# Forgetting attention: the decay bias of a whole PSUM bank by one 512-column product, and the gates' running sums in float32r parts

## The chip, the cores and the metric

The kernel runs on one core of a Trainium2 chip. The metric is the device time of one execution in microseconds (us), taken over three runs. Beside them one execution was recorded by the hardware profiler; all durations below come from it.

## The reference

The program is a decoder trunk of two layers on one sequence of 256 positions and 1024 channels, in float32. Each layer is a first SwiGLU step, a mixer and a second SwiGLU step. The mixer projects the normed input once and runs three branches on the result: sparse attention (A), forgetting attention (B) and a gated delta rule (C). Each branch is projected, weighted by its gate, and the sum is projected back.

```
def forgetting_attention(q, k, v, log_f):            # 8 heads of 64
    c = transpose(cumsum(log_f, axis=1), (0, 2, 1))
    def block(args):                                 # 2 blocks of 128 queries
        qb, cb, pb = args
        logits = (einsum('bqhd,bshd->bhqs', qb, k) * d ** -0.5
                  + (cb[..., :, None] - c[..., None, :]))
        causal = pos[None, :] <= pb[:, None]
        p = softmax(where(causal, logits, -inf), axis=-1)
        return einsum('bhqs,bshd->bqhd', p, v)
```

The forget gates `log_f` (8 per position) are summed along the sequence, and the difference of the sums is added to the logits. The term of the query is the same for a whole row of the softmax and drops out of it; so the kernel adds only the key's term, −c[s].

## The kernel before, in words

**Matrix products.** The large products (`pw`, `po` of the SwiGLU steps; `pt`, the mixer's input projection; `pbr`, the branch projections; `pmo`, the output projection) take float32 weights that stream from HBM as `raw` tiles. ACT rounds each to float32r (`hi`) and DVE makes the rest (`lo`); TensorE multiplies hi·hi, lo·hi and hi·lo. These splits are issued at high priority.

**Branches.** `branch_a`, `branch_b` and `branch_c` are Python generators; the products of the projection are emitted one by one, and between them the generators are advanced a step at a time by a running estimate of time (`PACE`, `CP`, the `cost` of each product). The order in which each engine finally takes its instructions is set by a scheduler that simulates the engines. It cannot be read from the text alone: an instruction that was emitted a little later, or estimated a little longer, may end up far from where it was. The gate products (`pt`, six pieces of a 512-column projection) and the branch projections come in the order `SEQ`: gates 0 and 1, branch 0, gates 2, branch 1, branch 2.

**Branch B.** `branch_b` (line 945) first sums the gates: `lf` holds them on positions, and two float32 products with a triangle of ones, `tri1`, put the running sums of all 256 positions into the bank `cc`. DVE rounds them to `cq`, and makes `cr`, in which rows 0 to 7 hold the rounded sums of the 8 heads and rows 8 to 15 the rest, with a second copy at rows 64 to 79. Then `softmax_pv` (line 790) runs three jobs: the first block of queries with all four pairs of heads (128 keys), and the second block with pairs 0 and 1, and with pairs 2 and 3 (256 keys). A job has two banks of logits, `lg`: heads of even number in one, of odd number in the other, 512 columns each. `score` adds one head: a float32 product of q and k on 64 of the 128 rows (`lg<-bqk`; even heads use rows 0 to 63 and odd heads rows 64 to 127), then a float32r product on the same 64 rows that adds −c (`lg<-cr,ohr`), where `ohr` has −1 in the rows of the head. After that come the mask (DVE), the maximum, exp, sum and scaling (`L`, DVE and ACT), in the next steps the transposes of the probabilities (`pT`, copied to `PT` by ACT) and the value products (`pv`, 64-column stationary), and the parts `yh` (ACT) and `yl` (DVE) that the branch projection takes. The pool `pa` has two banks; `cc`, `lg`, `pT` and `pv` share them.

**Branch C.** The delta rule goes through four chunks; its last products are `wv`, added to `X` on DVE. Then ACT squares and sums `X` by head (`junk`, `so`), POOL raises the sum to −1/2, DVE scales `X` eight times, TensorE transposes it (`yc`), and ACT and DVE make its parts `ych` and `ycl`.

In the profile nearly every operation of ACT, DVE and POOL has line 85, every product line 147 and every transpose line 151, since helpers issue them; tiles tell them apart.

Of the kernel before, what the change touches and what calls it, by code (L numbers as in the profile page):

```python
# [9 lines left out]
F32 = mybir.dt.float32  # L10
F32R = mybir.dt.float32r
AF = mybir.ActivationFunctionType
OP = mybir.AluOpType
AX = mybir.AxisListType

P = 128
D = 1024
T = 256
# [15 lines left out]
C_ID, C_TRI, C_MASK, C_MASKT, C_LVL = 0, 128, 384, 640, 768  # L34
C_ROPE = C_LVL + 128 * len(LEVELS)
C_SEL = C_ROPE + 32
C_D16 = C_SEL + 10
C_O16 = C_D16 + 128
C_E16 = C_O16 + 128
N_CONST = C_E16 + 16  # L40
# [153 lines left out]
def trunk_kernel(ctx: ExitStack, tc: tile.TileContext, x, consts, par, rows, bgate, fnorm,  # L194
# [4 lines left out]
    cp = ctx.enter_context(tc.tile_pool(name="cp", bufs=1))  # L199
    rawp = ctx.enter_context(tc.tile_pool(name="rawp", bufs=NR))  # L200
    hlp = ctx.enter_context(tc.tile_pool(name="hlp", bufs=NH))
    wk = ctx.enter_context(tc.tile_pool(name="wk", bufs=2))
# [22 lines left out]
    E = Emit(tc, rawp, hlp, units, NR, NH)  # L225
    V, S, G = E.V, E.S, E.G
# [12 lines left out]
    cst = cp.tile([P, N_CONST], F32, name="cst")  # L239
# [4 lines left out]
    tri1 = cst[:, C_TRI:C_TRI + 2 * P]  # L244
    ones = cst[:, C_TRI + P:C_TRI + 2 * P]
    mask = cst[:, C_MASK:C_MASK + 2 * P]
# [2 lines left out]
    V.memset(mhalf, -0.5)  # L249
    phalf = cp.tile([P, 8], F32, name="phalf")  # L250
    V.memset(phalf, 0.5)
    ohr = cp.tile([P, 8], F32R, name="ohr")
    V.tensor_copy(ohr, cst[:, C_SEL + 2:C_SEL + 10])

    def k4(name, dt=F32):
        return wk.tile([P, 1024], dt, name=name, tag="k4", bufs=K4)
# [16 lines left out]
    def v3(t, a):  # L273
        return t.rearrange("p (a b) -> p a b", a=a)
# [197 lines left out]
    def k2(name):  # L472
        return wk.tile([P, 512], F32, name=name, tag="k2", bufs=K2)

    def tiny(name, n, bufs=2):
        return wk.tile([P, n], F32, name=name, tag="t_" + name, bufs=bufs)

    def rows_bc(r, name):

# [77 lines left out]
    def branch_c(l, qkv, gd, hh, hl, need):  # L557
# [101 lines left out]
        for t in range(2):  # L659
            V.tensor_tensor(half(Z, t).rearrange("p (q k r) -> p q k r", q=4, k=8),  # L660
                            zv[:, 4 * t:4 * t + 4, None, :].to_broadcast([P, 4, 8, 16]),
                            cst[:, None, C_D16:C_D16 + P].rearrange("p o (k r) -> p o k r", k=8).to_broadcast([P, 4, 8, 16]),
                            op=OP.mult)
# [122 lines left out]
            G.tensor_tensor(out=x1, in0=r[0], in1=r[1], op=OP.subtract)  # L786
            G.tensor_tensor(out=x2, in0=r[2], in1=r[3], op=OP.add)

    def softmax_pv(br, bias, score, pv, hh, hl):

        jobs = ((0, 0, 4), (1, 0, 2), (1, 2, 2))
        rows = (slice(0, 64), slice(64, 128))
        pr, ptt = {}, {}

        def logits(j):
            b, p0, npair = jobs[j]
            n = P * (b + 1)
            L = k4("L")  # L800
            lv = L.rearrange("p (h s) -> p h s", s=n)
            nh = 2 * npair
            mx, rs = tiny("mx", 8, 3), tiny("rsum", 8, 3)
            pts = [pa.tile([P, npair, n], F32, name="lg", tag="s") for _ in range(2)]
            for i in range(npair):
                for g in range(2):
                    score(pts[g][:, i, :], rows[g], p0 + i, g, b, i == 0)
            for g in range(2):
                V.tensor_tensor(lv[:, g * npair:(g + 1) * npair, :], pts[g],
                                bias(b)[:, None, :].to_broadcast([P, npair, n]), op=OP.add)  # L810
            V.tensor_reduce(mx[:, :nh], lv, axis=AX.X, op=OP.max, negate=True)
            for h in range(nh):
                S.activation(lv[:, h, :], lv[:, h, :], AF.Exp, bias=mx[:, h:h + 1],
                             accum_out=rs[:, h:h + 1])
            V.reciprocal(rs[:, :nh], rs[:, :nh])
            for h in range(nh):
                S.activation(lv[:, h, :], lv[:, h, :], AF.Copy, scale=rs[:, h:h + 1])
            pr[j] = lv

        def transposes(j):  # L820
            b, p0, npair = jobs[j]
            lv = pr.pop(j)
            ptt[j] = []
            for kb in range(b + 1):
                for h0 in range(0, 2 * npair, 4):
                    pt = pa.tile([P, 512], F32, name="pT", tag="s")
                    for h in range(4):
                        E.tr(pt[:, h * P:(h + 1) * P], lv[:, h0 + h, kb * P:(kb + 1) * P], ident)
                    o = k2("PT")
                    S.activation(o, pt, AF.Copy)  # L830
                    ptt[j].append(o)

        def values(j):
            b, p0, npair = jobs[j]
            pts = ptt.pop(j)
            pt = pa.tile([P, npair, P], F32, name="pv", tag="s")
            for kb in range(b + 1):
                if b == 0:
                    pe, po = pts
                else:  # L840
                    pe, po = pts[kb][:, :2 * P], pts[kb][:, 2 * P:]
                pv(pt, rows, pe, po, p0, npair, kb, kb == 0, kb == b)
            if j == 0:
                hh[br], hl[br] = ktiles("yh", 1)[0], ktiles("yl", 1)[0]
            d = (slice(None), slice(p0, p0 + npair), slice(b * P, (b + 1) * P))
            S.activation(hh[br][d], pt, AF.Copy)
            V.tensor_tensor(hl[br][d], pt, hh[br].bitcast(F32)[d], op=OP.subtract)

        n = len(jobs)
        for i in range(n + 2):  # L850
            if i < n:
                logits(i)
                yield
            if 0 <= i - 1 < n:
                transposes(i - 1)
                yield
            if 0 <= i - 2 < n:
                values(i - 2)
                yield
# [85 lines left out]
    def branch_b(gd, bq, bk, bv, hh, hl, after):  # L945
        E.finish(after)
        pt = pa.tile([P, 512], F32, name="cc", tag="s")
        lf = v3(gd["lf"], 2)
        E.mm(pt[:, 0:T], lf[:, 0, :], tri1, True, False, cost=0.434)
        E.mm(pt[:, P:T], lf[:, 1, :], tri1[:, :P], False, True)  # L950
        cr = wk.tile([P, T], F32R, name="cr", tag="cr", bufs=1)
        cq = wk.tile([P, T], F32R, name="cq", tag="cq", bufs=1)
        ct = wk.tile([P, T], F32, name="ct", tag="ct", bufs=1)
        V.tensor_copy(cq, pt[:, 0:T])
        V.tensor_scalar(ct, cq.bitcast(F32), cst[:, C_SEL:C_SEL + 1], None, op0=OP.mult)
        V.scalar_tensor_tensor(cr, pt[:, 0:T], cst[:, C_SEL + 1:C_SEL + 2], ct,
                                       op0=OP.mult, op1=OP.subtract)
        yield
        qv, kv, vv = v3(bq, 4), v3(bk, 4), v3(bv, 2)

        def score(o, rr, p, g, b, first):
            n = P * (b + 1)
            h = 2 * p + g
            E.mm(o, qv[rr, p, b * P:(b + 1) * P], kv[rr, p, :n], first, False, cost=0.217 * (b + 1))
            E.mm(o, ohr[rr, h:h + 1].to_broadcast([64, P]), cr[rr, :n], False, True, cost=0.109)

        def pv(pt, rows, pe, po, p0, npair, kb, first, last):
            for i in range(npair):
                for g, m in enumerate((pe, po)):
                    h = 2 * (p0 + i) + g  # L970
                    E.mm(pt[rows[g], i, :], vv[:, kb, 64 * h:64 * h + 64], m[:, i * P:(i + 1) * P],
                         first and i == 0, last, cost=0.135)

        yield from softmax_pv(1, lambda b: mask[:, P * (1 - b):], score, pv, hh, hl)

    def mixer(pi, st):
        xt, ssq, tasks = st
# [134 lines left out]
    first = new_xt()  # L1112
# [21 lines left out]
def shape_consts():  # L1134
    c = np.zeros((P, N_CONST), np.float32)
    i = np.arange(P)
    c[:, C_ID:C_ID + P] = np.eye(P)
    c[:, C_TRI:C_TRI + P] = i[:, None] <= i[None, :]
    c[:, C_TRI + P:C_TRI + 2 * P] = 1.0
    c[:, C_MASK + P:C_MASK + 2 * P] = np.where(i[None, :] <= i[:, None], 0.0, NEG)  # L1140
    c[:, C_MASKT:C_MASKT + P] = np.where(i[None, :] >= i[:, None], 0.0, NEG)
    for n, b in enumerate(LEVELS):
        bj, bi = i[:, None] // b, i[None, :] // b
        m = (bj % 2 == 0) & (bi == bj + 1)
        c[:, C_LVL + n * P:C_LVL + (n + 1) * P] = m.T
    c[:, C_D16:C_D16 + P] = i[:, None] // 16 == i[None, :] // 16
    c[:, C_O16:C_O16 + P] = c[:, C_D16:C_D16 + P] - np.eye(P)
    c[:, C_E16:C_E16 + 16] = i[:, None] % 16 == i[None, :16]
    pos = np.arange(T, dtype=np.float32)
    inv = np.power(np.float32(500000.0), -np.arange(0, 16, 2, dtype=np.float32) / np.float32(16))  # L1150
    ang = (pos[:, None] * inv[None, :]).astype(np.float32)
    for t in range(2):
        c[:, C_ROPE + 8 * t:C_ROPE + 8 * (t + 1)] = np.cos(ang[t * P:(t + 1) * P])
        c[:, C_ROPE + 16 + 8 * t:C_ROPE + 16 + 8 * (t + 1)] = np.sin(ang[t * P:(t + 1) * P])
    for r in (0, 64):
        c[r:r + 8, C_SEL] = -1.0
        c[r + 8:r + 16, C_SEL:C_SEL + 2] = 1.0
        for h in range(8):
            c[r + h, C_SEL + 2 + h] = -1.0
            c[r + 8 + h, C_SEL + 2 + h] = -1.0  # L1160
    return c


# [38 lines left out]
```

## Time and profile before

| | |
|---|---|
| three runs | 1135.08, 1137.55, 1138.8 us (median 1137.55) |
| profiled execution | 1136.66 us, span 1134.8 us |
| TensorE (PE) | 1110.2 us busy, 98% |
| VectorE (DVE) | 814.0 us, 72% |
| ScalarE (ACT) | 659.0 us, 58% |
| GpSimd (POOL) | 94.4 us, 8% |
| mean granted TensorE clock | 0.995 |
| HBM | 170 GB/s over the span |

A share of busy time is a mean over stages with different limits. Rows of a timeline give start, length, engine, line, operation, output and inputs, shape; in square brackets stands the idle time of the engine just before, with what ended it. A float32 product appears as two records; ends of products are modelled and overlap, so the pace is read from one start to the next. Layer 0's branch B lies at about 330 to 385 us of the span, layer 1's some 560 us later.

### The profile page before, as it was taken

The numbers are of one execution on the slowest core, as the hardware profiler recorded it, in microseconds if no ns is written. First come the engines' busy times: TensorE is split into PE (matmuls) and PEld (weight loads), VectorE is DVE, ScalarE is ACT, GpSimd is POOL, SyncE is SP. The second block draws the span as 40 slices with busy tenths as digits, with TensorE's granted clock in tenths as the row PEclk, the third lists the DMA queues.
The fourth block names the chain that finished last, engine by engine and source line by source line (L and its number), as shares of the span: only waits on it lengthen the run. The fifth ranks groups of instructions, "written<-read, shape, count | busy, mean of one in ns | idle before, by whom it ended". The sixth has DMA issues, their size and how long they took to land. (4 is left out here: it accounts for less than half of the span.)

```text
span 1134.8 us, 17281 instructions
## 1 busy us (share of the span) xinstructions
PE 1110.2 (98%) x6540; PEld 947.5 (83%) x6540; DVE 814.0 (72%) x1328; ACT 659.0 (58%) x1164; POOL 94.4 (8%) x116
## 2 busy tenths in 40 slices
PE   7999999998999999999999999999999999999997
PEld 6888898897778788888888888989878778788885
DVE  5777579889746676776567766888896557677764
ACT  6665456644758646655456645565647685465643
POOL 0010002100000100100010100030000002010100
PEclk9999999999999999999999999999999999999999
DMA  7666656555434355666656666564554334556662
GB/s 280 192 187 187 188 174 190 166 160 167 151 111 148 119 182 154 202 188 189 188 180 186 186 193 188 170 186 154 165 170 155 103 111 149 182 162 191 187 208 91
DMA packets 56515, 194.08 MB, mean 171 GB/s; under 512 B 6256, under 2 KB 8816, under 8 KB 56432
## 3 DMA queue, kind: packets, MB, share of 16 engines
q1 hardware_dynamic: 56144, 192.46, 54.9%
q8 instruction: 51, 0.84, 0.3%
q10 hardware_dynamic: 288, 0.52, 0.1%
q14 instruction: 32, 0.26, 0.1%
HBM read 191.78 MB, written 1.18 MB: 170 GB/s over the span
## 5 line engine op out<-in xcount | busy, mean ns | idle before, releaser
L85 DVE TENSOR_TENSOR lo<-raw,hi 128x1024 fp32r<-128x1024 f32 (+2 forms) x353 | 444.6, 1260 | 218.1 <-ACT hi L85 214.5
L85 ACT ACTIVATE hi<-raw 128x1024 fp32r<-128x1024 f32 (+2 forms) x353 | 372.7, 1056 | 322.3 <-PE pt L147 86.5
L147 PE MATMUL pw<-xt,hi 128*128 128x512 f32 x1024 | 352.2, 399 | 4.1 <-ACT hi L85 2.5
L147 PE MATMUL pw<-xt,lo 128*128 128x256 f32 x1024 | 265.0, 281 | 0.0
L147 PEld LDWEIGHTS pw<-xt,hi 128*128 128x128 f32 x1024 | 189.9, 189 | 43.0 <-ACT hi L85 3.2
L147 PE MATMUL pt<-hi,xt 128*128 128x512 f32 (+1 forms) x640 | 207.0, 399 | 4.7 <-DVE gate L85 4.7
L147 PEld LDWEIGHTS pw<-xt,lo 128*128 128x128 f32 x1024 | 193.7, 189 | 8.3
L147 PEld LDWEIGHTS pt<-hi,xt 128*128 128x128 f32 x640 | 120.5, 190 | 29.6 <-issue 6.2
L147 PE MATMUL pt<-lo,xt 128*128 128x512 f32 (+1 forms) x320 | 128.4, 401 | 1.7 <-DVE lo L85 1.7
L147 PE MATMUL pt<-xt,hi 128*128 128x256 f32 x640 | 118.0, 286 | 0.0
L147 PE MATMUL po<-hi,hl 128*128 128x512 f32 x256 | 99.9, 390 | 0.0
L147 PE MATMUL po<-lo,hh 128*128 128x512 f32 x256 | 99.7, 389 | 0.0
L147 PEld LDWEIGHTS pt<-xt,hi 128*128 128x128 f32 x640 | 99.1, 191 | 0.4
L147 PE MATMUL po<-hi,hh 128*128 128x512 f32 x256 | 91.1, 390 | 0.0
L147 PE MATMUL pt<-xt,lo 128*128 128x256 f32 x320 | 88.9, 284 | 0.0
L147 PEld LDWEIGHTS pt<-lo,xt 128*128 128x128 f32 x320 | 61.1, 191 | 14.8 <-DVE lo L85 2.6
L85 POOL TENSOR_TENSOR hr<-hg,rbc 128x512 f32<-128x512 f32 x32 | 43.2, 1349 | 313.5 <-DVE hg L85 293.9
L147 PEld LDWEIGHTS pt<-xt,lo 128*128 128x128 f32 x320 | 60.5, 191 | 0.0
L147 PEld LDWEIGHTS po<-hi,hl 128*128 128x128 f32 x256 | 48.1, 188 | 9.9
L147 PEld LDWEIGHTS po<-hi,hh 128*128 128x128 f32 x256 | 48.1, 188 | 9.8
L147 PEld LDWEIGHTS po<-lo,hh 128*128 128x128 f32 x256 | 48.1, 188 | 9.8
L85 ACT ACTIVATE hh<-hu 128x512 fp32r<-128x512 f32 x32 | 20.2, 631 | 24.7 <-DVE hu L85 24.7
(249 smaller groups left out, 1346.1 us busy)
## 6 DMA issues: line engine op xcount, KB each, us to landing
raw<-in_wmx SPq DMA_DIRECT2D x112, 512.0 KB, 3.6
raw<-in_wf2i SPq DMA_DIRECT2D x64, 512.0 KB, 4.1
raw<-in_wf1i SPq DMA_DIRECT2D x63, 512.0 KB, 4.0
raw<-in_wf1o SPq DMA_DIRECT2D x32, 512.0 KB, 4.1
raw<-in_wf2o SPq DMA_DIRECT2D x32, 512.0 KB, 4.2
raw<-in_wbr SPq DMA_DIRECT2D x24, 512.0 KB, 3.3
raw<-in_wmo SPq DMA_DIRECT2D x16, 512.0 KB, 4.1
raw<-in_wms SPq DMA_DIRECT2D x8, 468.0 KB, 3.9
```

Source lines behind the costliest of these rows:

```text
L85: return f(*args, **kw)
L147: self.nc.tensor.matmul(out, lhsT, rhs, start=start, stop=stop, skip_group_check=True)
```

## The change

Two things, both for `branch_b`.

The running sums: `lf` is split into a float32r part `lfh` (ACT) and the rest `lfl` (DVE), and the sums are four float32r products with `tri1r`, a rounded copy of the triangle, that DVE makes once at the start.

The bias: `cr` becomes a float32 tile, and ACT makes from it `crp`, four scaled copies of 128x256, one for each pair of heads; the scale keeps the rows of that pair and sets all others to zero. `ohr` has two columns, −1 in the rows of the even and of the odd heads. At the start of a job `forget` puts one float32r product of 512 columns into each of the two banks, on all 128 rows, and this gives the bias of all heads of that bank; `score` then only adds q·k. `crp` takes one more tile of the pool `k4`, from which the 128x1024 tiles of the mixer come.

```diff
-    ohr = cp.tile([P, 8], F32R, name="ohr")
-    V.tensor_copy(ohr, cst[:, C_SEL + 2:C_SEL + 10])
+    ohr = cp.tile([P, 2], F32R, name="ohr")
+    V.tensor_copy(ohr, cst[:, C_SEL + 6:C_SEL + 8])
+    tri1r = cp.tile([P, 2 * P], F32R, name="tri1r")
+    V.tensor_copy(tri1r, tri1)
...
-    def softmax_pv(br, bias, score, pv, hh, hl):
+    def softmax_pv(br, bias, score, pv, hh, hl, bank_first=None):
...
             pts = [pa.tile([P, npair, n], F32, name="lg", tag="s") for _ in range(2)]
+            if bank_first is not None:
+                for g in range(2):
+                    bank_first(pts[g], g, b, p0, npair)
             for i in range(npair):
                 for g in range(2):
                     score(pts[g][:, i, :], rows[g], p0 + i, g, b, i == 0)
...
     def branch_b(gd, bq, bk, bv, hh, hl, after):
         E.finish(after)
         pt = pa.tile([P, 512], F32, name="cc", tag="s")
-        lf = v3(gd["lf"], 2)
-        E.mm(pt[:, 0:T], lf[:, 0, :], tri1, True, False, cost=0.434)
-        E.mm(pt[:, P:T], lf[:, 1, :], tri1[:, :P], False, True)
-        cr = wk.tile([P, T], F32R, name="cr", tag="cr", bufs=1)
+        lf = gd["lf"]
+        lh, ll = tiny("lfh", 256, 1, F32R), tiny("lfl", 256, 1, F32R)
+        S.activation(lh, lf, AF.Copy)
+        V.tensor_tensor(ll, lf, lh.bitcast(F32), op=OP.subtract)
+        for tb in range(2):
+            for i, a in enumerate((lh, ll)):
+                E.mm(pt[:, tb * P:T], v3(a, 2)[:, tb, :], tri1r[:, :T - tb * P], tb == 0 and i == 0, tb == 1 and i == 1,
+                     cost=0.11)
+        cr = wk.tile([P, T], F32, name="cr", tag="cr", bufs=1)
...
+        crp = v3(k4("crp", F32R), 4)
+        for p in range(4):
+            S.activation(crp[:, p, :], cr, AF.Copy, scale=cst[:, C_SEL + 2 + p:C_SEL + 3 + p])
         yield
...
+        def forget(pt, g, b, p0, npair):
+            E.mm(pt, ohr[:, g:g + 1].to_broadcast([P, P]), crp[:, p0:p0 + npair, :P * (b + 1)], True, False)
+
         def score(o, rr, p, g, b, first):
             n = P * (b + 1)
-            h = 2 * p + g
-            E.mm(o, qv[rr, p, b * P:(b + 1) * P], kv[rr, p, :n], first, False, cost=0.217 * (b + 1))
-            E.mm(o, ohr[rr, h:h + 1].to_broadcast([64, P]), cr[rr, :n], False, True, cost=0.109)
+            E.mm(o, qv[rr, p, b * P:(b + 1) * P], kv[rr, p, :n], False, True, cost=0.217 * (b + 1))
```

The constants lose two columns, and the selector's rows are laid out for the new scales. Since the scheduler works from the new instructions, the order of the other work on each engine changes as well, around branch B and behind it.

TensorE at the logits of block 1, pairs 0 and 1, in layer 0, before (`lg<-bqk` the score of a head, `lg<-cr,ohr` its bias, `st` the delta rule):

```order
L147 MATMUL lg<-bqk 128x256
L147 MATMUL lg<-cr,ohr 128x256
L147 MATMUL lg<-bqk 128x256
L147 MATMUL lg<-cr,ohr 128x256
L147 MATMUL lg<-bqk 128x256
L147 MATMUL lg<-cr,ohr 128x256
L147 MATMUL lg<-bqk 128x256
L147 MATMUL lg<-cr,ohr 128x256
L147 MATMUL st<-T_2830,kd 128x128 x4
```

TensorE at the same place now (`lg<-crp,ohr` the bias of a bank, `ks` and `qs` the delta rule):

```order
L147 MATMUL lg<-crp,ohr 128x512
L147 MATMUL lg<-bqk 128x256 x2
L147 MATMUL lg<-crp,ohr 128x512
L147 MATMUL lg<-bqk 128x256 x2
L147 MATMUL ks<-St,fmk 128x128 x4
L147 MATMUL qs<-St,fmq 128x128 x4
```

Before, heads of the one and of the other bank alternated; now both heads of the one bank come first, then both of the other.

TensorE at the end of the gate products in layer 0, before (`pt` gates, `wv` and `yc` delta rule, `pT` and `pv` transposes and values of the attention, `pbr` branch projections):

```order
L147 MATMUL pt<-hi_3927,xt 128x512
L147 MATMUL wv<-T_2830,wT 128x128 x4
L151 MATMUL pT<-ident,L 128x128 x4
L147 MATMUL pt<-lo_3928,xt 128x512
L147 MATMUL pt<-hi_3927,xt 128x512 x2
L147 MATMUL pt<-lo_3928,xt 128x512
L147 MATMUL pt<-hi_3927,xt 128x512 x2
L147 MATMUL pv<-PT,bv 64x128 x8
L147 MATMUL pt<-lo_3928,xt 128x512
L147 MATMUL pt<-hi_3927,xt 128x512 x2
L147 MATMUL pt<-lo_3928,xt 128x512
L147 MATMUL pv<-PT,bv 64x128 x8
```

TensorE at the same place now:

```order
L147 MATMUL pt<-lo_3931,xt 128x512
L147 MATMUL pt<-hi_3930,xt 128x512
L147 MATMUL wv<-T_2832,wT 128x128 x4
L147 MATMUL pv<-PT,bv 64x128 x8
L151 MATMUL pT<-ident,L 128x128 x8
L147 MATMUL pv<-PT,bv 64x128 x8
L151 MATMUL yc<-ident,X 128x128 x8
L147 MATMUL pbr<-hi_3948,yh 128x512
L147 MATMUL pbr<-lo_3949,yh 128x512
L147 MATMUL pbr<-hi_3948,yh 128x512
L147 MATMUL pbr<-lo_3949,yh 128x512
L147 MATMUL pv<-PT,bv 64x128 x8
```

Before, one more `pt`, 17 `pbr` and then the first `yc` followed. Now all gate products stand ahead of `wv`, and the eight `yc` ahead of the first `pbr` behind it.

ACT behind the delta rule's copy `T` in the same stretch, before (`hi` splits, `PT` copies of the transposes, `junk,so` square sums of the delta rule, `yh` and `ych` parts of branches B and C):

```order
L85 ACTIVATE T_2830<-vh 128x512
L85 ACTIVATE yh<-pv 128x4x128
L85 ACTIVATE hi_3945<-raw_3868 128x1024
L85 ACTIVATE PT<-pT 128x512
L85 ACTIVATE hi_3963<-raw_3886 128x1024
L85 ACTIVATE PT<-pT 128x512
L85 ACTIVATE junk,so<-X 128x128 x4
L85 ACTIVATE yh<-pv 128x2x128 x2
```

ACT now, a few rows behind `T`:

```order
L85 ACTIVATE hi_3966<-raw_3889 128x1024
L85 ACTIVATE hi_3991<-raw_3916 128x1024
L85 ACTIVATE PT<-pT 128x512
L85 ACTIVATE junk,so<-X 128x128 x3
L85 ACTIVATE PT<-pT 128x512
L85 ACTIVATE junk,so<-X 128x128
L85 ACTIVATE ych<-yc,cw 128x512 x2
L85 ACTIVATE yh<-pv 128x4x128
```

The `yh` of the first job stands behind `ych` now, and a `PT` stands between the square sums.

More of the change, by code (lines that the diff above doesn't have):

```diff
@@ L36 @@
 C_SEL = C_ROPE + 32
-C_D16 = C_SEL + 10
+C_D16 = C_SEL + 8
 C_O16 = C_D16 + 128
@@ L473, in k2, with tiny @@
         return wk.tile([P, 512], F32, name=name, tag="k2", bufs=K2)
-    def tiny(name, n, bufs=2):
-        return wk.tile([P, n], F32, name=name, tag="t_" + name, bufs=bufs)
+    def tiny(name, n, bufs=2, dt=F32):
+        return wk.tile([P, n], dt, name=name, tag="t_" + name, bufs=bufs)
     def rows_bc(r, name):
@@ L972, in pv @@
                          first and i == 0, last, cost=0.135)
-        yield from softmax_pv(1, lambda b: mask[:, P * (1 - b):], score, pv, hh, hl)
+        yield from softmax_pv(1, lambda b: mask[:, P * (1 - b):], score, pv, hh, hl, forget)
     def mixer(pi, st):
@@ L1157, in shape_consts @@
         c[r + 8:r + 16, C_SEL:C_SEL + 2] = 1.0
-        for h in range(8):
-            c[r + h, C_SEL + 2 + h] = -1.0
-            c[r + 8 + h, C_SEL + 2 + h] = -1.0
+    for h in range(8):
+        for i in (h, 8 + h):
+            c[i, C_SEL + 2 + h // 2] = 1.0
+            c[i, C_SEL + 6 + h % 2] = -1.0
     return c
```

## The prediction

> **What bounds the kernel now.** I read the page first, then the stretches of the span in which the forgetting attention runs (by engine), then what TensorE waits for, then the timeline of those stretches in both layers.
>
> ```profile
> span 1134.8 us, 17281 instructions
> PE 1110.2 (98%) x6540; PEld 947.5 (83%) x6540; DVE 814.0 (72%) x1328; ACT 659.0 (58%) x1164; POOL 94.4 (8%) x116
> PE 45%; DVE 2%; DMA 1%; ACT 0%; issue 0%; POOL 0%; POOLq 0%; DVEq 0%; ACTq 0%; SPq 0%
> ```
>
> TensorE is busy 98% of the span and carries 45% in the chain of waits, against 2% for the next engine. The time is the sum of TensorE's work and of the few holes in it: 24.6 us in all (1134.8 − 1110.2).
>
> ```profile
> 346.00:360.00 14.00, 14.00 (x81) 11.32 (x78) 6.53 (x10) 13.65 (x40) 0.00 (x0) 1.00 0.34 109
> 360.00:376.00 16.00, 16.00 (x97) 12.82 (x96) 9.33 (x13) 11.86 (x29) 0.00 (x0) 1.00 0.45 148
> 376.00:392.00 16.00, 16.00 (x103) 12.86 (x102) 10.59 (x21) 9.01 (x19) 3.60 (x3) 1.00 0.40 131
> 880.00:952.00 72.00, 72.00 (x444) 56.28 (x443) 42.17 (x61) 48.87 (x117) 4.20 (x3) 1.00 0.36 114
> ```
>
> The columns are length, then busy time of PE, its weight loads, DVE, ACT and POOL, the granted clock, the DMA share and GB/s. Where the changed products stand (346 to 392 in layer 0, 880 to 952 in layer 1) PE has no hole. ACT is full at 346 to 360 (13.65 of 14.00). So the edit counts on PE in two ways: what its products take there, and whether PE still finds work while the serial chains of the attention and of the delta rule run on ACT, DVE and POOL.
>
> **The change, part by part.** First the products, per layer.
>
> The sums over the gates go from two float32 products to four float32r ones.
>
> ```profile
> 331.37 0.67 PE L147 MATMUL lv<-Z,T 64*64 64x64 f32 x8
> 331.98 0.92 PE L147 MATMUL cc<-cst,lf 128*128 128x256 f32 x4
> 332.83 0.67 PE L147 MATMUL lv<-Z,T 64*64 64x64 f32 x8
> ```
>
> Four records, from 331.98 to the next work at 332.83: 0.85 us. A float32r product has one record. The trace has none of 256 columns at full height, so I take half of a 512-column one (0.23, next fence) for the 256-column ones and the same per column for the 128-column ones: 2 × 0.115 + 2 × 0.06 = 0.29 for the products, and about 0.35 of change of shape before and after stays (0.85 less some 0.5 for the four old records). Together 0.65: **−0.2**, bounds 0 and −0.5. The split of the gates into two parts is an ACT and a DVE operation on 128x256; it stands far ahead of branch B, and the new cast of the triangle on DVE stands at the start.
>
> The bias.
>
> ```profile
> 387.28 0.39 PE L147 MATMUL pbr<-hi,yh 128*128 128x512 f32 x1
> 387.50 0.39 PE L147 MATMUL pbr<-lo,yh 128*128 128x512 f32 x1
> 345.24 0.39 PE L147 MATMUL pt<-lo,xt 128*128 128x512 f32 x1
> 345.55 0.71 PE L147 MATMUL lg<-bqk 64*128 64x256 f32 x4
> 345.90 0.48 PE L147 MATMUL lg<-cr,ohr 64*128 64x256 f32 x2
> 346.86 1.16 PE L147 MATMUL st<-T,kd 128*128 128x128 f32 x8
> 357.22 0.84 PE L147 MATMUL pt<-hi,xt 128*128 128x512 f32 x3
> 357.99 0.70 PE L147 MATMUL lg<-bqk 64*128 64x256 f32 x2
> 359.28 0.50 PE L147 MATMUL pt<-lo,xt 128*128 128x512 f32 x1
> ```
>
> Starts, not durations, give the pace: a 512-column float32r product takes 0.23 us (387.28 to 387.50). The score products use half the rows. Four heads whose products alternate between both halves cost from 345.24 + 0.23 to 346.86, plus 0.1 at the exit: 1.5 us. Two heads on one half alone cost from 357.22 + 3 × 0.23 = 357.9 to 359.28, plus 0.1: also 1.5. So the halves overlap, and about 0.4 of each such block is the change of shape at its two ends (0.32 from 357.67 to 357.99 and 0.39 at the end, where like products would follow after 0.23 and 0.22, and some 0.1 at each first record).
>
> The Trainium skill, "TensorEngine Tiling (Array Packing)", Key Properties, says that changing the tiling mode, not only the tile, drains the engine. By that rule a full-height bias product between two half-height scores is the wrong neighbour. The trace agrees with about 0.4 us for a block.
>
> In the logits of block 1, pairs 0 and 1, the order shown with the change has four heads alternating between the halves before, and now bias, two heads of the one half, bias, two of the other. One bank is one half of the rows, so the four scores no longer overlap: two blocks where there was one. Each is 1.5 less two bias records of about 0.12 = 1.26, plus 0.23 for the bank's product: 2 × 1.49 = 3.0 against 1.5, **+1.5**. Pairs 2 and 3 were two single blocks already (3.0) and become 0.46 + one block of two heads and one of two with nothing between: about 2.6, **−0.4**. In block 0 eight bias records of some 0.06 each (they overlap in pairs) and one block's change of shape (0.4) go, and 2 × 0.23 come: **−0.4**. The value products (64-column shape) stand in four blocks per layer before, one of them alone, and in three after: **−0.4**. Sum of the products per layer: −0.2 + 1.5 − 0.4 − 0.4 − 0.4 = **+0.1, which I call nothing**, bounds −1.0 and +0.8. As a gain on PE the edit is worth nothing.
>
> **The load on ACT.** Four scaled copies of 128x256 come in, just ahead of the logits.
>
> ```profile
> 354.87 1.69 ACT L85 ACTIVATE L<-L,rsum 128x256 f32<-128x256 f32 x4
> ```
>
> By this row, the same operation on the same shape, they take 1.7 us. PE has other products ready for that time, so they cost nothing directly, but they push the softmax back, on the engine that is full at 346 to 360.
>
> **What moves.** Because the softmax of the third job (block 1, pairs 2 and 3) comes later, its probabilities are ready only when the last gate products are used up. In the order of TensorE at the end of the gate products (shown with the change; one more `pt`, 17 `pbr` and the first `yc` followed there before) the two chains meet. The filler between `wv` and `yc` is gone: eleven `pt` and 17 `pbr` products. On ACT, which serves both chains, the copies `PT` that `pT` and `pv` wait for now cut into the square sums `junk`, and `yh`, which the first `pbr` needs, stands behind `ych`, hence behind `yc`. In the order before, `yh` of the first job stood two large splits ahead of these. So PE, which takes its queue in order, must wait out the delta rule's chain.
>
> ```profile
> 377.53 1.05 PE L147 MATMUL wv<-T,wT 128*128 128x128 f32 x8
> 378.42 0.60 PE L151 MATMUL pT<-ident,L 128*128 128x128 f32 x4
> 378.62 0.69 DVE L85 TENSOR_TENSOR X<-X,wv 128x512 f32<-128x512 f32 x1 [2.00 <-PE wv L147]
> 379.05 0.60 ACT L85 ACTIVATE PT<-pT 128x512 f32<-128x512 f32 x1 [0.50 <-PE pT L151]
> 379.55 0.30 ACT L85 ACTIVATE junk<-X 128x128 f32<-128x128 f32 x1
> 379.97 0.31 ACT L85 ACTIVATE junk<-X 128x128 f32<-128x128 f32 x1
> 380.34 1.09 PE L147 MATMUL pv<-PT,bv 128*64 128x128 f32 x16
> 381.06 0.19 ACT L85 ACTIVATION_READ_ACCUMULATOR junk<-X 128x1 f32 x1
> 381.28 0.17 DVE L85 SCALAR_TENSOR_TENSOR so<-so,aq 128x8 f32<-128x8 f32 x1 [0.84 <-ACT junk L85]
> 381.52 1.64 POOL L85 TENSOR_TENSOR so<-so,mhalf 128x8 f32<-128x8 f32 x1 [144.44 <-DVE so L85]
> 383.20 2.19 DVE L85 SCALAR_TENSOR_TENSOR X<-X,so,zs 128x128 f32<-128x128 f32 x8 [0.88 <-POOL so L85]
> 387.74 0.27 PE L151 MATMUL yc<-ident,X 128*128 128x128 f32 x1
> 388.66 0.82 PE L151 MATMUL yc<-ident,X 128*128 128x128 f32 x6
> 389.19 1.26 ACT L85 ACTIVATE ych<-yc,cw 128x512 fp32r<-128x512 f32 x2 [1.33 <-PE yc L151]
> 373.81 0.60 ACT L85 ACTIVATE yh<-pv 128x512 fp32r<-128x512 f32 x1 [0.42 <-PE pv L147]
> ```
>
> Before, `wv` ends at 378.58 and X is scaled by 385.39, 6.8 us later; PE takes the first `yc` at 387.74 and waits for nothing. In the new order, from the end of `wv` (0): `pv` of the first job to 1.3 (1.1 and the change of shape); the first four `pT` to 1.8, their copy to 2.6; `junk` three times at 0.42 each to 3.9; the second copy, whose transposes ended at 3.2, to 4.5; the last `junk` to 5.0; `so` 5.3; POOL 6.9; X scaled eight times to 9.2; the last `yc` 9.5; the second `ych` 10.2; `yh` 10.8; first `pbr` **10.9**. PE's own work in it is 1.3 + 0.45 + 0.45 + 1.2 (`pv` of the second job) + 0.9 (`yc`) = 4.3. The rest, **6.6 us per layer**, is waiting, in four pieces: about 0.8 for the copy, 1.4 ahead of the second `pv`, 3 ahead of `yc`, 1.5 ahead of `pbr`. Lower bound: X as fast as before (6.8), `yc`, `ych` and `yh` 1.6 behind it: 8.4 − 4.3 = 4.1. Upper bound: the two splits `hi` ahead of `PT` on ACT, one at 1.06 by the row below, late: 8.
>
> ```profile
> 390.45 1.06 ACT L85 ACTIVATE hi<-raw 128x1024 fp32r<-128x1024 f32 x1
> ```
>
> What stands behind the waiting instruction is all that PE has left, `pbr` and `pmo`, so nothing makes up for it. Layer 1 has the same order.
>
> **The clock after a hole.**
>
> ```profile
> 272.78 0.39 PE L147 MATMUL pt<-hi,xt 128*128 128x512 f32 x1
> 275.53 0.47 PE L147 MATMUL pt<-hi,xt 128*128 128x512 f32 x1 [2.36 <-DVE gate L85]
> 276.30:279.70 3.40, 3.40 (x9) 2.65 (x8) 3.40 (x11) 0.41 (x1) 0.00 (x0) 0.51 0.69 196
> ```
>
> A hole of 2.4 us is followed by 3.4 us at a granted clock of 0.51: nine products there where the full pace of 0.23 fits fifteen, 1.5 to 1.7 us lost. The new holes together are longer and each shorter or about as long; I count 0.9 a layer, between 0 (none is long enough) and 1.7 (one window).
>
> The Trainium skill, "TensorE: Matmul & The Clock Gate", The HAM clock gate (the "warmup" mystery), puts the half clock behind at least one idle window of about 3.4 us. By it the holes of 3 us and less here would cost nothing more, and the total would be 1.8 us lower. The trace's hole of 2.4 us, with the half clock behind it, speaks for the higher one.
>
> **Sum.** 0 + 6.6 + 0.9 = 7.5 a layer, 15.0 in both. Against the profiled execution of before, 1136.7 us (1.9 around its span; 0.9 under the median 1137.55 of the three runs), this gives 1151.7; I say **1151**.
>
> **Rivals.** (1) The products alone count, since the chain's waits are covered after all (the profile of before has PE without a hole in these 118 us, and ACT 9.01 of 16.00 at 376 to 392 has room): between −1.0 and +0.8 a layer, so 1135 to 1138. Against it: the order of PE's queue is fixed and the filler is not in it. (2) Faster: the half-height blocks run closer together than in the trace (the bank's product overlaps the blocks beside it, and all four value blocks count), so the products give −2 a layer, and waits stay under 1: 1133. It needs the waits gone, and the rows 357.67 to 359.28 speak against the overlap. (3) Slower than my forecast: the chain's `PT` copies start behind late splits (+1.4, the upper bound of 8.0) and the half clock takes a whole window and a second one behind it in each layer (1.7 × 2): 8.0 + 3.4 = 11.4 a layer, 1159. It decides where the waits fall close together, within one window of 3.4 us. (4) Only ACT's load counts: the 1.7 us of copies pass through once a layer to PE, 1140.
>
> **How the numbers follow.** Forecast 0.70; (1) 0.08; (2) 0.04; (3) 0.10; (4) 0.08. A measurement of this kernel tells 0.3% (3.4 us) from no change. Faster: (2), 0.04. Within 0.3%, 1134.1 to 1141.0: (1) and most of (4), 0.13. Slower: 0.83. The forecast's own bounds are 4.1 + 0 − 1.0 and 8.0 + 1.7 + 0.8 a layer, 1143 to 1158; (4) pulls the low end to 1141, and half of (3) lies above 1157. Range 1141 to 1157.
>
> **What would show it.** PE idle in two stretches of about 11 us, one a layer, right behind the last gate product, with waits on ACT `PT`, on DVE `X` ahead of `yc`, and on ACT `yh` ahead of `pbr`: 12 to 14 us more of PE's waits in all; PE busy time within 3 us of 1110. The half clock would stand in the granted clock behind these stretches. The pace is wrong if two single-half blocks at pairs 0 and 1 take other than 3.0; the moved chain is wrong if `yc` follows `wv` by less than 8 us with no idle PE, and the whole is wrong if PE is full there.

## The result, and the profile after

| | before | changed |
|---|---|---|
| median of the runs | 1138.17 us (1135.08 to 1139.67, 4 runs) | 1152.68 us (1151.97 to 1155.08, 4 runs) |
| profiled execution: span | 1134.8 us | 1150.2 us |
| PE busy | 1110.2 us | 1114.4 us |
| mean granted clock | 0.995 | 0.991 |

The ratio is 1.0138, with a 95% interval of 1.012 to 1.0155: the changed kernel is 14.5 us slower. The forecast was 1151.

The page of the changed kernel, span, engines and the chain that ended last:

```profile
span 1150.2 us, 17257 instructions
PE 1114.4 (97%) x6520; PEld 948.7 (82%) x6520; DVE 816.1 (71%) x1331; ACT 663.3 (58%) x1174; POOL 98.1 (9%) x116
PE 44%; DVE 2%; ACT 1%; DMA 1%; POOL 0%; issue 0%; POOLq 0%; ACTq 0%; DVEq 0%
```

PE is still the bound by its share, and 97% against 98% looks like nothing. But PE idles 35.8 us of the span (1150.2 − 1114.4) where it idled 24.6 before, and its busy time grew by 4.2 us. What PE waits for, engine and line, us in total, times, longest:

```profile
PE xt L151 <- DMA xs<-in_x: 4.7, 3, 4.0
PE pt L147 <- DVE gate L85: 3.9, 2, 2.4
PE yc L151 <- DVE X L85: 3.8, 6, 1.5
PE ix L147 <- DVE qs L85: 3.6, 4, 2.4
PE pbr L147 <- ACT yh L85: 2.6, 2, 1.3
PE pv L147 <- ACT PT L85: 2.0, 2, 1.0
...
PE pT L151 <- ACT PT L85: 1.4, 2, 0.7
```

Four of these waits are new, each in both layers: `yc` for `X`, `pbr` for `yh`, `pv` and `pT` for `PT`, 9.8 us together. The wait `ix` for `qs` was 0.3 before; it hangs on a DMA (DVE idles 6.1 us for its tile `nb`, 3.2 before) and came out between 0 and 3.7 us in the later runs, in fast kernels too, so it is no part of the argument. The timeline of layer 0 shows the four in a row:

```profile
378.56 1.05 PE L147 MATMUL wv<-T,wT 128*128 128x128 f32 x8
...
381.91 0.66 PE L151 MATMUL pT<-ident,L 128*128 128x128 f32 x4 [0.69 <-ACT PT L85]
...
382.92 0.58 ACT L85 ACTIVATE PT<-pT 128x512 f32<-128x512 f32 x1
383.40 0.30 ACT L85 ACTIVATE junk<-X 128x128 f32<-128x128 f32 x1
383.55 1.09 PE L147 MATMUL pv<-PT,bv 128*64 128x128 f32 x16 [0.99 <-ACT PT L85]
...
385.74 2.19 DVE L85 SCALAR_TENSOR_TENSOR X<-X,so,zs 128x128 f32<-128x128 f32 x8 [1.76 <-POOL so L85]
386.15 0.33 PE L151 MATMUL yc<-ident,X 128*128 128x128 f32 x1 [1.51 <-DVE X L85]
...
389.14 0.86 ACT L85 ACTIVATE yh<-pv 128x512 fp32r<-128x512 f32 x2
389.78 0.79 PE L147 MATMUL pbr<-hi,yh 128*128 128x512 f32 x1 [1.27 <-ACT yh L85]
390.37 0.63 PE L147 MATMUL pbr<-lo,yh 128*128 128x512 f32 x1
390.80 0.63 PE L147 MATMUL pbr<-hi,yh 128*128 128x512 f32 x1
```

From the end of `wv` (379.61) to the first `pbr` (389.78) pass 10.2 us. The chain is the one that the prediction followed: `PT`, three `junk`, `PT`, `junk`, the power on POOL, `X`, `yc`, `ych`, `yh`. The last two rows stand 0.43 apart, where like products stand 0.23 apart. That is the half clock, and the stretches of both layers show it (length, busy time of PE, its weight loads, DVE, ACT and POOL, clock, DMA share, GB/s):

```profile
258.18:261.60 3.42, 3.03 (x7) 1.84 (x7) 3.35 (x7) 3.10 (x9) 0.00 (x0) 0.50 0.29 63
384.48:387.89 3.41, 1.51 (x10) 0.78 (x7) 2.15 (x8) 0.06 (x1) 1.23 (x1) 1.00 0.02 6
387.89:391.30 3.41, 2.14 (x7) 1.38 (x6) 2.45 (x5) 2.33 (x5) 0.00 (x0) 0.50 0.00 0
391.30:394.72 3.42, 3.42 (x21) 2.42 (x20) 0.42 (x1) 0.39 (x1) 0.00 (x0) 0.50 0.00 0
951.09:954.50 3.41, 1.77 (x8) 0.95 (x8) 2.19 (x8) 0.60 (x2) 0.69 (x1) 1.00 0.02 6
954.50:957.91 3.41, 2.21 (x6) 1.37 (x8) 2.34 (x4) 1.43 (x4) 0.00 (x0) 0.50 0.02 5
957.91:961.33 3.42, 3.42 (x20) 2.80 (x19) 0.43 (x1) 0.39 (x1) 0.00 (x0) 0.50 0.00 0
```

Each layer has two whole windows of 3.41 us at half clock behind its holes. A fifth (258.18) lies behind the `ix` wait. Half of PE's busy time in them is lost: (3.03 + 2.14 + 3.42 + 2.21 + 3.42) / 2 = 7.1 us. The kernel before had two such windows, filled by PE, 3.4 us.

That gives an account that all later runs are read by: **span = PE's work at full clock + what the half clock took + PE's idle time**. Before it is 1106.8 + 3.4 + 24.6, after 1107.3 + 7.1 + 35.8. The products cost 0.5 us more, the clock 3.7, the holes 11.2: together 15.4, the difference of the spans.

One part of the clock is missing in this account. The clock is on record only from 10.7 to 15.7 us into the span on, by the execution, and the work takes PE to run at full clock ahead of that. The rows of the start say otherwise; in the kernel before the record begins at 13.42:

```profile
12.66 0.63 PE L147 MATMUL pw<-xt,hi 128*128 128x512 f32 x1
13.09 0.41 PE L147 MATMUL pw<-xt,lo 128*128 128x256 f32 x1
...
15.40 0.40 PE L147 MATMUL pw<-xt,hi 128*128 128x512 f32 x1
15.64 0.40 PE L147 MATMUL pw<-xt,lo 128*128 128x256 f32 x2
```

The product behind a `hi` of 512 columns comes after 0.43 us there and after 0.24 later on. So the work contains, as an estimate, half of PE's busy time ahead of the record: 3.7 us before (7.39 / 2), 3.4 in the change, and between 2.5 (e3) and 5.0 (e5) in the runs. It lies ahead of all that the edits change and differs by the execution. The column "less start" takes it out; by it the products of the change cost 0.8 us more, not 0.5.

### The profile page after: what moved, and what is told of

Its sections match the earlier page's. It is cut to its first block, busy times and chain, and to the rows that moved or that the text cites. A ratio compares the mean times of both kernels' runs of the same rounds, so it can differ in the third digit from the quotient of the medians.

```text
span 1150.2 us, 17257 instructions
## 1 busy us (share of the span) xinstructions
PE 1114.4 (97%) x6520; PEld 948.7 (82%) x6520; DVE 816.1 (71%) x1331; ACT 663.3 (58%) x1174; POOL 98.1 (9%) x116
## 5 line engine op out<-in xcount | busy, mean ns | idle before, releaser
L147 PE MATMUL pt<-hi,xt 128*128 128x512 f32 (+1 forms) x640 | 203.1, 393 | 3.9 <-DVE gate L85 3.9
L85 ACT ACTIVATE hh<-hu 128x512 fp32r<-128x512 f32 x32 | 20.2, 633 | 24.6 <-DVE hu L85 24.6
```

The source lines that it names most:

```text
L85: return f(*args, **kw)
L147: self.nc.tensor.matmul(out, lhsT, rhs, start=start, stop=stop, skip_group_check=True)
```

## The experiments

Theory 1: the time goes where the new order leaves the delta rule's chain without other products on TensorE. Theory 2: the new products cost it, by their shapes. Theory 3: the copies `crp` cost it, by their load on ACT. Times are medians, each with its ratio to the kernel before as run beside it. The account is that of each profiled execution; "less start" is the work without the estimate for the start, and the last column counts how often PE's array changes its shape from one product to the next (the work follows this count only loosely: e5 has the fewest and needs more than e4).

| run | median us | ratio (95%) | work | less start | half clock | idle | shape changes |
|---|---|---|---|---|---|---|---|
| before | 1138.17 | 1 | 1106.8 | 1103.1 | 3.4 | 24.6 | 102 |
| the change | 1152.68 | 1.0138 (1.012 to 1.0155) | 1107.3 | 1103.9 | 7.1 | 35.8 | 98 |
| e1, sums alone | 1133.53 | 0.9973 (0.9958 to 0.9989) | 1104.6 | 1100.1 | 1.7 | 26.2 | 94 |
| e2, bias alone | 1136.45 | 0.9997 (0.9987 to 1.0007) | 1106.0 | 1103.4 | 1.7 | 26.3 | 98 |
| e3, copies alone | 1132.70 | 0.9959 (0.9944 to 0.9975) | 1102.6 | 1100.1 | 1.7 | 27.1 | 94 |
| e4, change, CP 0.8 | 1126.87 | 0.9911 (0.9896 to 0.9927) | 1102.7 | 1099.3 | 0.0 | 21.2 | 80 |
| e5, before, CP 0.8 | 1155.10 | 1.0179 (1.0165 to 1.0193) | 1107.5 | 1102.5 | 6.4 | 39.4 | 77 |
| e6, copies on POOL | 1138.51 | 1.0034 (1.0022 to 1.0045) | 1106.6 | 1103.3 | 3.2 | 26.7 | 94 |
| e7, holes filled | 1151.32 | 1.0133 (1.0111 to 1.0155) | 1111.6 | 1107.9 | 3.4 | 32.7 | 100 |
| e8, `yc` two steps later | 1135.50 | 0.9986 (0.9974 to 0.9999) | 1105.9 | 1103.1 | 1.7 | 26.5 | 98 |

The kernel before had a median of 1136.15 beside e1 to e4, 1134.90 beside e5 to e7 and 1137.09 beside e8.

### e1, e2, e3: one part alone

e1 keeps the change's sums (`lfh`, `lfl`, `tri1r`) and the old bias; e2 keeps the bias and the old sums. e3 changes no product of the kernel before and only adds work on ACT:

```diff
                                        op0=OP.mult, op1=OP.subtract)
+        crp = v3(k4("crp"), 4)
+        for p in range(4):
+            S.activation(crp[:, p, :], cr.bitcast(F32), AF.Copy, scale=cst[:, C_SEL + 1:C_SEL + 2])
         yield
```

> The running sums in float32r parts alone; the bias stays one product a head, and nothing is added on ACT but one copy a layer. Theory 1 (the time is lost where the new order leaves the delta rule's chain without other products on TensorE): in this order 36 gate products stand between wv and yc, but yc stands ahead of the first pbr, and yh behind ych; small waits at yc and pbr, 1 to 2 us a layer, so +1 to +4 us against before (1139 to 1142). Theory 2 (the products themselves cost, through their shapes): the sums gain 0.2 a layer, 1137.8. Theory 3 (ACT's copies crp cost): no copies here, no change, 1138.

> The bias of a bank alone, with its four copies on ACT; the running sums stay float32. Theory 1: here 31 gate products stand between wv and yc, and pv, pT stand between them; waits below 1 us a layer, no half clock: within 3 us of before (1137 to 1141). Theory 2: all products of the bias are as in the change, so nearly its whole loss stays, 1150 or more. Theory 3: all copies are there, so the loss stays, 1150 or more.

> The kernel before with four copies of 128x256 added on ACT behind cr that nobody reads; no product is changed. Theory 1: the order moves by these copies alone and yc comes ahead of pbr again; two or three waits at yc, 2 us a layer, +2 to +5 us (1140 to 1143). Theory 2: no product has changed, so no change, 1138. Theory 3: the whole loss of the change, 1150 or more.

None of the three is slower than before. e2 has all products of the bias and all copies, and no loss: against theories 2 and 3. e3 has the load without the loss, again against theory 3. For e1 and e3 theory 1 expected a few us more and got 2.6 and 3.5 less: the order had been read for where `yc` stands and not for when its chain starts. In neither did `yc` wait at all; `pbr` in e1 waited 0.5 us a layer for `yh`. What e3 gained stands mostly in its work, 1100.1 against 1103.1 less the start, with the same products. TensorE of e3 at pairs 2 and 3 of block 1:

```profile
359.84 0.39 PE L147 MATMUL pt<-hi,xt 128*128 128x512 f32 x1
360.15 0.81 PE L147 MATMUL lg<-bqk 64*128 64x256 f32 x3
...
361.78 0.50 PE L147 MATMUL pt<-hi,xt 128*128 128x512 f32 x1
```

The four heads stand in one block here, 360.15 to 361.78, 1.6 us. In the kernel before they are two blocks of 1.3 us each, apart from each other. That saves 1.0 us a layer, and the value products, in three blocks of 1.02 us where they took 3.42 in four, 0.36: 2.6 of the 3.0 us. e1 has the same blocks of scores. So the order moves PE's work itself, with the products of the change between 1099.3 (e4) and 1103.9, and a part that only adds load can make the kernel faster.

### e4, e5: the pace of the delta rule

```diff
-CP = 0.6
+CP = 0.8
```

e4 is this edit on the change, e5 on the kernel before.

> The whole change, with one number of the order altered: the pace CP of the delta rule's generator 0.8 and not 0.6. The same products, copies and splits; in the order 22 pbr products stand between wv and yc now, and yh ahead of them. Theory 1: the waits at PT, X and yh and the half clock behind them are gone, and what the products save shows: 1133 to 1138, as fast as before or a little faster. Theories 2 and 3: nothing that they count has changed, 1150 to 1153.

> The kernel before with the delta rule's pace CP 0.8 and no part of the change: the control of the run before this, whose 1127 us is 9 us under the kernel before. Theory 1 (order alone): the 2.4-us hole at the gates and the half clock behind it go in both layers here as well (2 x about 4 us); but in this order lv, vh, st, wv, ks and qs follow each other with no other product between, so PE waits for ACT's copies there, 2 to 4 us a layer: 1131 to 1138. Theory 2 (the change's products save what showed there): this kernel keeps the old products, so it stays at 1136 to 1138, and the whole difference of 9 us is the change's. If the pace alone gives all the gain: 1127.

e4 has every product and copy of the change and is 0.9% faster than before, the fastest kernel of this study. So neither the products (theory 2) nor the copies (theory 3) explain the loss of the change by themselves. It went further than theory 1 said, since a wait that the kernel before has is gone as well. What PE waits for in e4:

```profile
PE xt L151 <- DMA xs<-in_x: 4.5, 3, 3.9
PE pw L147 <- ACT hi L85: 1.6, 2, 1.1
PE pmo L147 <- ACT mh L85: 1.5, 2, 0.8
PE st L147 <- ACT T L85: 1.5, 2, 0.7
```

The wait of `pt` for `gate`, 4.7 us before, is not there, and behind the start no window with work of PE is at half clock. e5 shows that the pace alone is no gain: 1155 us, where theory 1 had said 1131 to 1138. In its order `yc` stands 18 `pbr` behind `wv`, but the chain behind `wv` takes longer than these: in layer 0, on DVE `so` stands behind `gate` and `mtmp`, on POOL the power behind a `mrg`, and `yc` starts 12.6 us after `wv`. What PE waits for in e5, its longest entry:

```profile
PE yc L151 <- DVE X L85: 14.5, 2, 7.2
```

These are 7.2 us in each layer, at the place where the change waits, with none of the change's products. The place and the mechanism are theory 1's; how long each hole gets was not foreseen. Of e4's gain over before (10.9 us of span) 3.8 are work, 0.3 the start, 3.4 half clock and 3.4 idle time; how much of it the old products would gain under a like order, no run shows.

### e6: the copies on POOL

```diff
-            S.activation(crp[:, p, :], cr, AF.Copy, scale=cst[:, C_SEL + 2 + p:C_SEL + 3 + p])
+            G.tensor_scalar(crp[:, p, :], cr, cst[:, C_SEL + 2 + p:C_SEL + 3 + p], None, op0=OP.mult)
```

> The whole change, pace 0.6 as in it, but the four scaled copies crp run on POOL, not on ACT. Products and splits are unchanged. In its order 26 pbr and pv stand between wv and yc. Theory 1: the waits of the change at PT, X and yh go, the gate hole stays as before: 1133 to 1138. Theory 2: the products are those of the change, 1150 to 1153. Theory 3 (ACT's load): the load is off ACT, so 1138 or a little less, as in theory 1; it differs from theory 1 in that e3 should then have been slow.

The loss is gone to within 3.6 us, and so are the four waits; 1138.5 lies 0.5 us above theory 1's range. Its account differs from that of before by +2.1 us of idle time, since the `ix` wait is 3.4 us longer in this execution and others are shorter, and by nothing in work. By itself e6 would fit theory 3 too. With e3, which has the copies on ACT and is fast, it does not.

### e7: the holes filled

Four products without use go ahead of `yc`; they read the square sums, so they are ready when POOL starts. The power then writes another tile.

```diff
+        so1 = so
+        so = tiny("so2", 8)
-        G.tensor_tensor(out=so, in0=so, in1=mhalf, op=OP.pow)
+        G.tensor_tensor(out=so, in0=so1, in1=mhalf, op=OP.pow)
...
+            if j == 0:
+                for _ in range(4):
+                    nc.tensor.matmul(pt[:8, 0, :], so1, zs[:, :T], start=True, stop=True, skip_group_check=True)
```

> The change in its slow order, with four products without use (256 columns, float32, 8 stationary columns, 1.7 us) put on TensorE in the wait ahead of yc; the square sums' power goes to a tile of its own for it. Waits and their ends are as in the change (first yc within 0.3 us of it). If the half clock behind the holes costs 2 us a layer as the trace shows, and if it is set by how idle one window of 3.4 us is, one or both half-clock windows a layer go: 1147 to 1151. If the clock does not matter or the idle share of a window does not set it: 1152 to 1154. With the rule that only a hole of a whole window counts, the half clock of the change itself would not be there.

Behind the holes, the two windows of layer 0 became one and those of layer 1 went. With one more at the gates (279.07) and none at `ix`, the half clock took 3.4 us in all, not 7.1. The window ahead of `yc` in layer 0 of e7 and the two behind it:

```profile
384.90:388.31 3.41, 3.18 (x26) 1.68 (x26) 1.15 (x5) 0.47 (x3) 1.64 (x1) 1.00 0.16 62
388.31:391.72 3.41, 1.90 (x9) 1.23 (x10) 2.79 (x8) 2.17 (x5) 0.00 (x0) 1.00 0.00 0
391.72:395.13 3.41, 3.41 (x20) 2.34 (x20) 0.75 (x2) 0.39 (x2) 0.00 (x0) 0.50 0.00 0
```

Filled, the window is followed by full clock; the next, with PE busy for 1.90 us (at `yc` and the wait for `yh`), is followed by half clock. This fits a clock that goes by what PE did in the window before. The median, 1151.3, lies between the two ranges that were expected. It is 1.4 us under that of the change, by the ratios to before only 0.6, and its runs spread from 1145.4 to 1152.8; the intervals of e7 and of the change overlap. By the accounts, less the start, the useless products took 4.0 us of work where the idle time fell by 3.1. The clock's part is thus shown in the windows, and only weakly in the time.

### e8: `yc` two steps later

```diff
+        yield
+        yield
         yield
         for j in range(2):
             pt = pc.tile([P, 2, T], F32, name="yc", tag="s")
```

> The change as it is, with two empty steps more in the delta rule's generator ahead of yc, so that yc is issued two steps later. No product, copy or split differs, and up to the last wv every engine's order is that of the change; behind it, 16 pbr stand between wv and yc again, and yh ahead of ych. Theory 1 (the loss is the place of yc and yh): the waits at PT (1.7 a layer), X (1.9) and most of that at yh (1.3) go, and with them the four half-clock windows; some 1 to 1.5 us a layer stays (PT, yl): 1152.7 less 11 to 14, 1138 to 1142. Theory 2 (products, shapes) and theory 3 (ACT's copies): nothing they count differs, 1150 to 1154. If only the clock went: 1147.

This is the change with only the issue of `yc` moved. Of the 6520 instructions of PE 84 stand at another place than in the change, of ACT's 1174 only 19, all of them behind `wv`. The whole loss is gone: 1135.5 us, ratio 0.9986 (0.9974 to 0.9999). TensorE of e8 in layer 0:

```profile
376.58 1.05 PE L147 MATMUL wv<-T,wT 128*128 128x128 f32 x8
...
379.35 0.50 PE L147 MATMUL pbr<-hi,yh 128*128 128x512 f32 x1
...
383.73 0.40 PE L147 MATMUL pbr<-hi,yl 128*128 128x512 f32 x1
384.06 1.09 PE L147 MATMUL pv<-PT,bv 128*64 128x128 f32 x16
...
386.11 0.27 PE L151 MATMUL yc<-ident,X 128*128 128x128 f32 x1
```

`yc` comes 9.5 us behind the start of `wv`, and no row between them has an idle time: PE does `pv`, `pT` and `pbr` in that stretch. None of the four new waits is left. Less the start, work is 1103.1 against the change's 1103.9 and the same as before; idle time is 26.5 against 35.8, the half clock 1.7 against 7.1. Theory 1 holds, and it had been too careful: no 1 to 1.5 us a layer stayed. The edit moves `yc` behind 16 `pbr` and `yh` ahead of `ych` at once; which share of the loss is whose, no run shows.

## Why the prediction was right, and where its terms were off

**The sign and the cause held.** PE idles behind the last gate product in both layers, in the four waits that were named, in their order, and e8 shows that the place of `yc` and `yh` in the order, taken together, is the cause of the whole loss.

**The waits: 6.6 us a layer.** Measured are 4.9 (0.69, 0.99, 1.51 + 0.20 + 0.20 and 1.27 in layer 0). The chain took 10.2 us from `wv` to `pbr` where 10.9 had been counted. The piece ahead of `yc` was taken as 3 us and is 1.9, since `yc` follows `X` head by head: the first starts 0.4 us after the first scaling begins and does not wait for the eighth. From there on PE counts mostly as busy.

**The clock: 0.9 us a layer.** Mis-sized. Each layer got two whole windows at half clock; they took 2.8 us a layer ((2.14 + 3.42) / 2 and (2.21 + 3.42) / 2). Against that, both windows of the kernel before (3.4 us) are gone and one came behind the `ix` wait (1.5), so 3.7 us net over both layers, against 1.8 forecast. The forecast did not count that those two windows would go; without that the term would have been off by more. Its reading of one window was off by a little too: nine products where fifteen fit at 0.23 are 1.4 us lost, not 1.5 to 1.7; half of the busy time of a full window gives the 1.7.

**The products: +0.1 us a layer, called nothing.** Measured is +0.8 us over both (less the start), and 0.0 in e8, which has the same products. That it is about nothing held; not all terms did. Terms: the sums from 0.85 to 0.61 us, −0.24 (−0.2 forecast). Pairs 0 and 1, TensorE of the changed kernel:

```profile
345.53 0.39 PE L147 MATMUL pbr<-lo,yh 128*128 128x512 f32 x1
345.76 0.40 PE L147 MATMUL lg<-crp,ohr 128*128 128x512 f32 x1
346.08 1.13 PE L147 MATMUL lg<-bqk 64*128 64x256 f32 x4
347.14 0.49 PE L147 MATMUL lg<-crp,ohr 128*128 128x512 f32 x1
347.57 1.13 PE L147 MATMUL lg<-bqk 64*128 64x256 f32 x4
348.62 0.60 PE L147 MATMUL ks<-St,fmk 128*128 128x128 f32 x3
```

From 345.76 to 348.62 are 2.86 us; with the change of shape at the end 3.0, as forecast, against 1.5. The two banks do run one behind the other, and their scores no longer overlap. Pairs 2 and 3 and block 0 gained less than forecast (0.14 and 0.17 us a layer, measured from the first to the next other product, against 0.4 each). With all three the logits take 7.04 us a layer, against 5.78 before: as a product, the bias of a bank costs more than the bias by heads here. The value products stand in three blocks, as forecast; at full clock, in e8, these take 3 × 1.02 us, against 3.42 before: −0.36 (−0.4 forecast). The terms come to +0.66 a layer. The whole measures 0.3 (the change) to 0.7 (e8) a layer less; where in PE's other work that lies stays open.

**The rest.** 9.8 of the 11.2 us of additional idle time are the four waits; the `ix` wait (+3.3) is set off by shorter waits at `gate`, `lo` and the first `hi`. The waits were forecast 3.4 us too high over both layers, the clock 1.9 too low and the products 0.6, and the rest of the idle time was not forecast at all. That these errors cancel is luck; it brought the sum to within 2 us of the measured median.

**What moved the order** was put down to the four copies on ACT in the prediction ("they push the softmax back"). That is half shown: with the copies on POOL the order is good (e6), but with the copies alone (e3) or with the copies and the new bias (e2) it is good too. At this pace, only the sums, the bias and the copies on ACT together gave this order. No single part of the edit carries it.

## What to carry to other kernels

Where a scheduler sets the order, a small edit is not costed by its own instructions: the same products gave 1127, 1135.5, 1138.5 and 1153 us under four orders. Follow each long serial chain on other engines (here from the start of `wv` to `yc`, 7.6 us in the change and 12.6 in e5) and count the independent products that the new queue leaves beside it; and count from the time at which the chain starts, not only by its place. A hole costs its length and, where it left its window of the clock nearly idle, the half clock behind it. Here the mend was to issue the waiting instruction later, two lines.

## What the runs showed of the hardware

The windows of half clock start on a fixed raster of 3.41 us within an execution, and they follow windows in which PE was busy for a short time. In ten traces, between the first record of the clock and the last products, all 15 windows of the raster with PE busy for up to 1.5 us were followed by half clock, and none with more than 2.3 us. Between these, some were and some were not: in e7 one with 1.90 us was and one with 1.92 was not, so the busy time is not the whole measure. So the same hole can be free or cost 1.7 us by where it falls. The wait for `gate` of 2.35 us in e8, in layer 0 first, then in layer 1:

```profile
270.96:274.38 3.42, 2.52 (x12) 1.75 (x10) 3.42 (x9) 1.76 (x2) 0.00 (x0) 1.00 0.52 158
274.38:277.79 3.41, 1.95 (x9) 1.63 (x10) 3.41 (x9) 1.47 (x3) 0.00 (x0) 1.00 0.68 217
277.79:281.20 3.41, 3.41 (x17) 2.82 (x16) 3.41 (x11) 0.69 (x1) 0.00 (x0) 1.00 0.67 197
830.75:834.16 3.41, 1.06 (x6) 0.59 (x4) 3.41 (x10) 1.24 (x2) 0.00 (x0) 1.00 0.70 177
834.16:837.58 3.42, 3.42 (x9) 2.65 (x9) 3.42 (x10) 1.08 (x2) 0.00 (x0) 0.50 0.67 220
```

In layer 0 the raster cuts the hole in two (PE busy 2.52 and 1.95), and the clock stays; in layer 1 it lies inside one window (1.06), and the next is at half clock, nine products instead of seventeen. The kernel before had the same hole at 1.05 and 1.32 in its windows and paid in both layers.

The Trainium skill, "TensorE: Matmul & The Clock Gate", The HAM clock gate (the "warmup" mystery), describes such a free-running window of about 3.4 us, and half clock after at least one idle one. The raster agrees with the traces; an idle window need not be empty, since 1.5 us of work in 3.41 did not keep the clock.
